# Mixture-of-experts stage of a hybrid decoder block: every expert in blocks of 64 tokens on fp16 halves, weights split one expert ahead

## Chip, cores and metric

The kernel runs on 1 core of a Trainium2 chip. The metric is the device time of one execution in microseconds; of the kernel before there are three runs, and their median counts.

## The reference

One decoder layer over 1024 tokens of width 1024: a mixer (pooling and a state-space scan), then a hierarchical mixture of experts, then a final norm. Only the expert part is touched here. Each token goes to 2 of 32 experts, and an expert is a SwiGLU network with an inner width of 512:

```python
def expert_block(args):
    xb, e = args                       # tokens of expert e
    hu = xb @ w13[e]                   # (n, 1024) @ (1024, 1024)
    a_, b_ = jnp.split(hu, 2, axis=-1)
    return (jax.nn.silu(a_) * b_) @ w2[e]      # (n, 512) @ (512, 1024)
...
out = jax.ops.segment_sum(ys * row_w[:, None], row_tok, num_segments=T)
```

Everything is float32. The router run on the given inputs puts these numbers of tokens on experts 0 to 31: 7, 16, 9, 6, 33, 30, 44, 11, 77, 47, 11, 29, 109, 27, 54, 2, 397, 71, 32, 31, 120, 163, 183, 41, 34, 55, 111, 35, 54, 49, 112, 48. In blocks of 64 that is one block for 23 experts, two for e8, e12, e17, e20, e26 and e30, three for e21 and e22, and seven for e16: 48 blocks, 16 of them behind an expert's first.

## The kernel before

All stages run one after the other; the expert stage is the last long one, a Python loop `for e in range(NE)` written out for 32 experts. The order of instructions on each engine is the order of the code (no scheduler works here), and each engine meets the branches on the token count `rv` by itself.

Weights. An expert has 12 chunks of 512 KB: eight of `w13` (128 rows of the 1024 x 1024 matrix each) and four of `w2`. SP (SyncE) loads them with `load_to` into a ring of `NR` = 39 slots of [128, 1024] float32, 3.25 experts. `Q` = 4 keeps four loads in flight by a dependence, which `lds.clear()` resets. A load waits until the instructions that used its slot are done.

Tokens. The rows of a block are gathered by GpSimd (`gather`, two experts ahead for block 0), transposed by TensorE (`transposed`, tile `px`), and copied by ScalarE to `xa` in float32 (`prep`) or split into fp16 halves `xh` (`parts`).

Halves. A float32 operand can be written as a high and a low fp16 half, `hi = fp16(s*x)` on ScalarE and `lo = fp16(s*x - hi)` on VectorE (`split`, L55 to L59). A product is then three fp16 matmuls (`PASS`): hi by hi, hi by lo, lo by hi.

An expert with at most 64 tokens takes the Else arm (L1287 on): `up64` multiplies `xa` by the raw weights in float32 (64 matmuls of 256 columns), `gated` makes silu times gate (ScalarE, then VectorE, for each half `j`), `turned` transposes that and prepares the next expert's tokens, `refill` gives SP the next eight loads. [...] An expert's block 0 is weighted (`weigh`, VectorE, tile `ye`) and added to the result (`scatter_some`, GpSimd) inside the next expert's turn (`settle`).

An expert with more tokens takes the then-arm (L1264 on): it splits its eight `w13` chunks there, into `P` (two spare slots and its own raw slots, two chunks behind), multiplies two blocks at once with 48 fp16 matmuls of 512 columns (`up128s`), and goes into nested branches (L1282, then `more` with L1221 and L1235) for further pairs; an odd block uses `up64s` (96 fp16 matmuls of 256 columns).

## Time and profile before

| | us |
|---|---|
| median of 3 runs | 1235.07 (1225.71 to 1244.08) |
| profiled execution, own time | 1233.29 |
| its span in the trace | 1231.4 |
| PE (TensorE) busy | 1018.3, 83% |
| DVE (VectorE) busy | 547.8, 44% |
| ACT (ScalarE) busy | 393.0, 32% |
| moved by DMA | 302.82 MB, mean 246 GB/s |
| mean granted TensorE clock | 0.927 of full speed |

The times of all views are microseconds from the start of the span. PE is TensorE's matmul, PEld its weight load, SP the engine that issues the loads. The expert stage fills the stretch from about 534 to 1198; the final norm follows it. A share of busy time over the whole span mixes it with the stages ahead, so the stage is read in stretches of its own.

### The profile page before, as it was taken

The page shows a single profiled execution, that of the slowest core. Times are in us where ns is not written, and L with a number is a line of the kernel's source. Part 1 is how long each engine was busy: PE and PEld are TensorE (multiplying, and loading weights), DVE is VectorE, ACT ScalarE, POOL GpSimd, SP SyncE. Part 2 cuts the span into 40 slices and gives each one's busy share as a digit, 9 for nine tenths or more (in the row PEclk, how much of TensorE's full clock was granted, in tenths as well). Part 3 has the DMA queues.
Part 4 walks back from the last instruction along what each step waited for, and adds up shares of the span by engine and source line. Part 5 has one row for each costly group of instructions (what it writes and reads, how often), then busy time and mean ns, then how long its engine had stood idle before and what let it go on. Part 6 is the DMA issues. An engine that isn't in the chain of part 4 may idle for free.

```text
span 1231.4 us, 20504 instructions
## 1 busy us (share of the span) xinstructions
PE 1018.3 (83%) x7296; PEld 562.5 (46%) x7296; DVE 547.8 (44%) x1168; ACT 393.0 (32%) x747; POOL 253.3 (21%) x253
## 2 busy tenths in 40 slices
PE   4998988989898999667889787789888897797880
PEld 3433435666577555434444443434433343444440
DVE  6763669695788666710004041041413541040325
ACT  6434545465444322200114031041313431140312
POOL 1024324222220103311112121221122211211210
PEclk9998988999999999779989899899988999998995
DMA  9677773132201974789999999995789877999827
GB/s 315 198 193 189 222 226 79 37 80 44 60 1 53 373 283 148 291 275 365 356 355 355 361 374 360 368 367 187 231 272 365 310 233 217 340 369 366 307 31 281
DMA packets 115915, 302.82 MB, mean 246 GB/s; under 512 B 13556, under 2 KB 46506, under 8 KB 115602
## 3 DMA queue, kind: packets, MB, share of 16 engines
q1 hardware_dynamic: 96224, 259.83, 58.3%
q0 software_dynamic: 18160, 39.21, 13.9%
q8 instruction: 111, 1.82, 0.6%
q14 instruction: 202, 1.65, 0.4%
q10 hardware_dynamic: 1218, 0.31, 0.1%
HBM read 275.23 MB, written 24.07 MB: 243 GB/s over the span
## 4 chain that ended last, share of the span: by engine, by line
DMA 36%; PE 34%; issue 13%; DVE 10%; ACT 3%; POOL 2%; POOLq 1%; another core or an unknown queue 0%; DVEq 0%; SPq 0%; ACTq 0%
PE p L53 14%; DMA acc<-ye,idx 13%; DMA xg<-h2tab,idx 13%; PE proj L53 6%; PE po L53 5%; PE zp L53 3%; DMA abc<-acsd 2%; DMA table<-ent,dsti 1%; DMA wo<-in_w_dram 1%; DMA win<-in_w_ada_dram 1%; PE st L53 1%; PE pl L53 1%; DVE raw L1318 1%; DMA xt<-in_x_dram 1%; PE py L53 1%
## 5 line engine op out<-in xcount | busy, mean ns | idle before, releaser
L53 PE MATMUL proj<-hT,whl 128*128 128x512 f16 x768 | 182.9, 391 | 3.4 <-ACT hT L359 1.9
L1160 POOL DMA_INDIRECT acc<-ye,idx x48 | 74.1, 1543 | 238.9 <-DVE ye L1145 173.2
L53 PEld LDWEIGHTS <-whl 128*128 128x128 f16 x768 | 75.3, 100 | 103.4 <-issue 27.7
L1093 ACT ACTIVATE wp<-p 128x128 f32<-128x128 f32 (+1 forms) x37 | 11.4, 309 | 347.7 <-PE p L53 347.7
L1067 POOL DMA_INDIRECT xg<-h2tab,idx x48 | 51.4, 1070 | 312.9 <-PE p L53 176.5
L1145 DVE SCALAR_TENSOR_TENSOR ye<-p,gate,g2h 128x512 f32<-128x512 f32 x48 | 36.0, 750 | 175.1 <-PE p L53 145.2
L53 PE MATMUL p<-raw,xa 128*64 128x256 f32 x600 | 80.4, 421 | 28.3 <-issue 20.4
L53 PEld LDWEIGHTS <-xh 128*128 128x128 f16 (+1 forms) x816 | 66.7, 103 | 78.5 <-issue 10.5
L1094 DVE SCALAR_TENSOR_TENSOR wp<-p,wp 128x128 f32<-128x128 f32 (+1 forms) x37 | 12.3, 331 | 202.0 <-ACT wp L1093 195.3
L53 PEld LDWEIGHTS p<-raw,xa 128*64 128x64 f32 x600 | 54.9, 152 | 55.7 <-issue 42.0
L53 PE MATMUL zp<-wz,hT 128*128 128x192 f16 x768 | 69.3, 247 | 3.6 <-ACT zt L528 3.6
L53 PEld LDWEIGHTS <-hT 128*128 128x128 f16 x768 | 63.9, 99 | 6.4 <-issue 5.7
L53 PE MATMUL p<-wo,xa 128*64 128x256 f32 x368 | 50.9, 431 | 18.6 <-issue 15.7
L53 PE MATMUL po<-wo,yT 128*128 128x512 f16 x252 | 56.9, 379 | 0.0
L1094 DVE SCALAR_TENSOR_TENSOR wr<-p,wr 128x128 f32<-128x128 f32 (+1 forms) x37 | 12.3, 331 | 95.8 <-ACT wr L1093 92.7
L53 PEld LDWEIGHTS p<-wo,xa 128*64 128x64 f32 x368 | 33.4, 154 | 35.7 <-issue 26.5
L53 PE MATMUL p<-raw,xh 128*128 128x512 f16 (+1 forms) x234 | 48.8, 366 | 0.0
L1073 PE MATMUL px<-identf,xg 128*128 128x128 f32 x204 | 30.8, 278 | 14.5 <-DMA xg<-h2tab,idx 14.5
L1093 ACT ACTIVATE wr<-p 128x128 f32<-128x128 f32 (+1 forms) x37 | 11.4, 309 | 97.0 <-PE p L53 96.9
L593 POOL TENSOR_TENSOR abc<-acs,negm 128x768 f32<-128x768 f32 x16 | 24.7, 1606 | 77.6 <-DVE mh L635 77.5
L53 PEld LDWEIGHTS <-yT 128*128 128x128 f16 x252 | 24.7, 100 | 26.3
L53 PE MATMUL p<-yb,xa 128*64 128x256 f32 x224 | 30.6, 410 | 5.3 <-DMA raw<-in_w_dram 3.0
(483 smaller groups left out, 1887.2 us busy)
## 6 DMA issues: line engine op xcount, KB each, us to landing
raw<-in_w_dram SPq DMA_DIRECT2D x160, 512.0 KB
wo<-in_w_dram SPq DMA_DIRECT2D x80, 512.0 KB
yb<-in_w_dram SPq DMA_DIRECT2D x60, 512.0 KB
win<-in_w_ada_dram SPq DMA_DIRECT2D x32, 512.0 KB
yps<-in_w_dram SPq DMA_DIRECT2D x20, 512.0 KB
xc<-in_w_dram SPq DMA_DIRECT2D x19, 512.0 KB
xt<-in_w_ada_dram SPq DMA_DIRECT2D x16, 512.0 KB
win<-in_w_in_dram SPq DMA_DIRECT2D x16, 512.0 KB
```

Source lines behind the costliest of these rows:

```text
L53: return PE.matmul(o, l, r, start=start, stop=stop, skip_group_check=True)
L593: G.tensor_tensor(abc.rearrange("p c (r l) -> p c r l", r=3), acs[:, q2, hs, None].to_broadcast([128, 2, 3, 128]), negm[:, None, None, :]. ...
L1067: lastg[0] = G.indirect_dma_start(out=xg, out_offset=None, in_=h2tab, in_offset=bass.IndirectOffsetOnAxis(ap=ix, axis=0))
L1073: PE.transpose(pv[:, k], xg[:, k * 128:(k + 1) * 128], identf)
L1093: A.activation(sils[j][:, 0:n], p1s[j][:, 0:n], AF.Silu, scale=scale)
L1094: V.scalar_tensor_tensor(sils[j][:, 0:n], p1s[j][:, n:2 * n], scale, sils[j][:, 0:n], op0=ALU.mult, op1=ALU.mult)
L1145: V.scalar_tensor_tensor(y, p2, gt, g2h, op0=ALU.mult, op1=ALU.mult)
L1160: G.indirect_dma_start(out=acc, out_offset=bass.IndirectOffsetOnAxis(ap=ix, axis=0), in_=y, in_offset=None, compute_op=ALU.add)
L1318: V.scalar_tensor_tensor(js[i], ts[i], frs[:, i:i + 1], fnw, op0=ALU.mult, op1=ALU.mult)
```

## The change

All experts now run on fp16 halves, in blocks of 64 tokens.

- `up` (96 fp16 matmuls of 256 columns for a block) takes the place of `up64`, `up64s` and `up128s`; `xa`, `prep`, `more`, `EARLY` and the pairs of blocks are gone.
- `divide(e, ks)` splits chunks of expert e. Chunks 0 to 3 of expert e+1 are split during expert e's block 0 (two ahead of `up`, two between its halves `j`), chunks 4 to 7 at the start of its own turn.
- The halves of a chunk go to a slot that was freed two `w13` chunks before it: `plane[i]` is that slot, `lane[i]` the slot into which load i goes. The number of slots stays the same.
- For every expert, block 0 is finished ahead of the branch. Further blocks are `extra(b)`, nested one in the other, each with a hint at its start for the next branch.
- The hint for the expert's own branch stands at the start of its turn and no longer ahead of `down`.
- All 12 loads of an expert are issued together at its end, in both arms (before: 8 ahead of `down`, 4 behind it).

```diff
     for e in range(NE):
-        W = [ring[(12 * e + k) % NR] for k in range(12)]
-        P = wh + [t.bitcast(F16).rearrange("p (a n) -> p a n", a=2) for t in W[:6]]
+        W = lane[12 * e:12 * e + 12]
+        P = halves(e)
...
+        aim(f"e{e}")
+        divide(e, range(4, 8))
+        if e + 2 < NE:
+            gather(e + 2, 0, tokens(e + 2))
+        if e > 0:
+            weigh(p2s[0], slots(0, e - 1)[1], ys[3 * (e % 2)])
+            scatter_some(e - 1, 0, ys[3 * (e % 2)])
+        divide(e + 1, range(2))
+        up(P, 0, lambda: divide(e + 1, range(2, 4)))
+        turned(gT[0], (lambda: parts(xg0[(e + 1) % 2], 0)) if e + 1 < NE else None)
+        down(W, p2s[0], gT[0])
         with tc.If(rv > 64, preferred_fallthrough_block=True, label=f"e{e}") as br:
-            aim(f"b{e}")
...
+            extra(1)
+            refill()
         with br.Else():
-            fetch_ahead()
-            settle()
-            up64(W, e in (0,))
-            turned(0, 1, nxt)
             refill()
-        lds.clear()
-        if e + 1 < NE:
-            aim(f"e{e + 1}")
-        down(W, p2s[0], 0)
-        load_to(12 * e + 12 + NR)
         lds.clear()
```

The new functions (`refill` now reads `load_to(12 * e + 12 + NR)`):

```python
    idle = list(spare)
    for i in range(12 * NE + 2 * NT + 1):
        lane.append(ring[i] if i < NR else plane[i - NR])
        if i < 12 * NE and i % 12 < 8:
            idle.append(lane[i])
            plane.append(idle.pop(0))
        else:
            plane.append(lane[i])
...
    def up(P, a0, mid=None):
        for j in range(2):
            for k in range(8):
                for n, (a, b) in enumerate(PASS):
                    for h in range(2):
                        mm(p1s[j][64 * h:64 * h + 64, 0:256], xh[a][:, k, a0, :], cols(P[k][:, b], 256 * h + 128 * j, 128),
                           k == 0 and n == 0, k == 7 and n == 2)
            gated(j, 128, INV)
            if mid and j == 0:
                mid()
...
        def extra(b):
            last = b == BLOCKS - 1
            if not last:
                aim(f"e{e}b{b + 1}")
                if b == 1:
                    maybe(e, 2)
                maybe(e, b + 2)
            if b == 1:
                parts(rows(e, 1), 1)
            up(P, 1)
            g, p = gT[b % 2], p2s[1 + b % 2]
            turned(g, None if last else lambda: parts(rows(e, b + 1), 1))
            down(W, p, g)
            put(b, p, ys[1 + b % 2])
            if not last:
                with tc.If(rv > 64 * (b + 1), preferred_fallthrough_block=True, label=f"e{e}b{b + 1}"):
                    extra(b + 1)
```

DVE, the turn of expert 1 when it has one block, before: `ye` is `weigh` of expert 0, `wp` and `wr` are the gated halves, and no chunk is split on this path.

```order
L1145 SCALAR_TENSOR_TENSOR ye_5277<-p_5271,gate_4029,g2h 128x512
L1058 UNCONDITIONAL_BRANCH x2
L1094 SCALAR_TENSOR_TENSOR wp<-p_5267,wp 128x128
L1094 SCALAR_TENSOR_TENSOR wr<-p_5268,wr 128x128
L1264 UNCONDITIONAL_BRANCH
L1171 UNCONDITIONAL_BRANCH
```

DVE, the turn of expert 1 now: rows of L59 of 128x1024 make the low half of a chunk (four of expert 1, then four of expert 2), and the one of L59 into `xh` is that of the next tokens.

```order
L59 SCALAR_TENSOR_TENSOR wo_3868<-wo_4049,wo_3868 128x1024
L59 SCALAR_TENSOR_TENSOR wo_3919<-wo_4053,wo_3919 128x1024
L1126 SCALAR_TENSOR_TENSOR ye_5272<-p_5269,gate_4029,g2h 128x512
L59 SCALAR_TENSOR_TENSOR wo_4049<-x_4044,wo_4049 128x1024
L1065 UNCONDITIONAL_BRANCH
L59 SCALAR_TENSOR_TENSOR wo_4053<-sc_4059,wo_4053 128x1024
L1100 SCALAR_TENSOR_TENSOR wp<-p_5266,wp 128x128
L59 SCALAR_TENSOR_TENSOR x_4044<-sh_4058,x_4044 128x1024
L59 SCALAR_TENSOR_TENSOR sc_4059<-h_4048,sc_4059 128x1024
L1100 SCALAR_TENSOR_TENSOR wr<-p_5267,wr 128x128
L59 SCALAR_TENSOR_TENSOR xh_5265<-px,xh_5264 128x8x64
L1237 COMPARE_AND_BRANCH
```

Eight low halves of 128x1024 and one of `xh` now stand on the path of every expert; two chunks of the next expert stand ahead of the first gated half and two ahead of the second.

PE, the end of expert 0 and the branch of expert 1, before: the last transposes (`pg`, `px`), the hint, `down` (four rows of four matmuls), the count, and the branch.

```order
L1132 MATMUL pg<-identf,wr 128x128
L1264 UNCONDITIONAL_BRANCH
L1171 UNCONDITIONAL_BRANCH
L1350 BRANCH_PREFETCH_HINT
L53 MATMUL p_5271<-raw_4019,vecs 32x512 x4
L53 MATMUL p_5271<-raw_4021,vecs 32x512 x4
L53 MATMUL p_5271<-raw_4020,onesf 32x512 x4
L53 MATMUL p_5271<-raw_4022,onesf 32x512 x4
L1194 TENSOR_LOAD cnt
L1264 COMPARE_AND_BRANCH
```

PE, the same place now, the end of expert 0's block 0: the branch is that of expert 0 itself, and behind it stands the further block.

```order
L1117 MATMUL pg<-identf,wr 128x128
L53 MATMUL p_5269<-raw_4019,vecs 32x512 x4
L53 MATMUL p_5269<-raw_4021,vecs 32x512 x4
L53 MATMUL p_5269<-raw_4020,onesf 32x512 x4
L53 MATMUL p_5269<-raw_4022,onesf 32x512 x4
L1237 COMPARE_AND_BRANCH
L1294 BRANCH_PREFETCH_HINT
L1083 MATMUL px<-identf,xg_5260 128x2x2x32 x2
```

The hint has gone from here; it now stands ahead of the whole block 0 (`up` with its 96 matmuls, the transposes and `down`).

SP, the end of an expert's loads, before: eight loads end the arm, four follow, and then the next expert's branch.

```order
L793 DMA wo_4053<-in_w_dram 128x1024
L1264 UNCONDITIONAL_BRANCH
L1171 UNCONDITIONAL_BRANCH
L1350 BRANCH_PREFETCH_HINT
L793 DMA xc_4045<-in_w_dram 128x1024
L793 DMA xc_4046<-in_w_dram 128x1024
L793 DMA g1b<-in_w_dram 128x1024
L793 DMA h_4047<-in_w_dram 128x1024
L1194 TENSOR_LOAD cnt
```

SP, the same place now: the twelve loads (here the last seven) end the arm.

```order
L794 DMA wo_3834<-in_w_dram 128x1024
L794 DMA wo_3868<-in_w_dram 128x1024
L794 DMA wo_3919<-in_w_dram 128x1024
L794 DMA xc_4045<-in_w_dram 128x1024
L794 DMA xc_4046<-in_w_dram 128x1024
L794 DMA g1b<-in_w_dram 128x1024
L794 DMA h_4047<-in_w_dram 128x1024
L1237 UNCONDITIONAL_BRANCH
L1294 BRANCH_PREFETCH_HINT
L1183 TENSOR_LOAD cnt
```

SP meets one group of loads per expert instead of two.

## Rows read from the trace of the kernel before

**Rows 1.** The page's slices: the span in 40, busy tenths of DMA.

```profile
DMA  9677773132201974789999999995789877999827
```

**Rows 2.** Waits of PE in 534:1200: us in total, times, longest.

```profile
PE p L53 <- issue: 66.6, 32, 4.8
PE p L53 <- DMA raw<-in_w_dram: 9.0, 3, 3.1
```

**Rows 3.** Timeline of PE, one-block experts e28 and e29, their first rows.

```profile
1133.40 1.12 PE L53 MATMUL p<-wo,xa 128*64 128x256 f32 x4 [2.88 <-issue]
...
1149.81 0.71 PE L53 MATMUL p<-x,xa 128*64 128x256 f32 x4 [3.06 <-issue]
```

**Rows 4.** Timeline of PE: a 64-token fp16 block of e16, e17's start.

```profile
865.99 0.52 PE L53 MATMUL p<-h,xh 128*64 128x256 f16 x6
...
870.27 1.15 PE L53 MATMUL p<-raw,xh 128*64 128x256 f16 x18
...
872.44 1.92 PE L53 MATMUL p<-raw,uinc 128*32 128x512 f32 x16
874.18 1.90 PE L53 MATMUL p<-raw,negm 128*32 128x512 f32 x16
...
886.13 0.60 PE L53 MATMUL p<-h,xh 128*128 128x512 f16 x2 [0.69 <-ACT xh L57]
```

**Rows 5.** PE's branches and hints: duration ns min/median/max, first and last start.

```profile
L1264 PEldq COMPARE_BRANCH  x1: 5221/5221/5221, 1144.4 to 1144.4; - x1
L1350 PEldq BRANCH_PREFETCH_HINT  x1: 36/36/36, 1142.9 to 1142.9; - x1
L1282 PEldq COMPARE_BRANCH  x14: 74/350/6014, 670.4 to 1176.2; - x14
L1350 PEldq BRANCH_PREFETCH_HINT  x1: 31/31/31, 655.3 to 655.3; - x1
```

**Rows 6.** Groups by form, 534:1200: busy us, mean ns of one, idle before.

```profile
L59 DVE SCALAR_TENSOR_TENSOR raw<-raw,raw 128x1024 f16<-128x1024 f32 x25 | 29.5, 1220 | 0.3 <-ACT raw L57 0.3
L57 ACT ACTIVATE raw<-raw 128x1024 f16<-128x1024 f32 x25 | 25.9, 1054 | 3.0 <-DVE raw L59 2.2 <-DVE sh L59 0.2
L1145 DVE SCALAR_TENSOR_TENSOR ye<-p,gate,g2h 128x512 f32<-128x512 f32 x48 | 36.0, 750 | 175.1 <-PE p L53 145.2 <-issue 20.7 <-DMA acc<-ye,idx 5.0
L59 DVE SCALAR_TENSOR_TENSOR xh<-px,xh 128x512 f16<-128x512 f32 x19 | 12.6, 686 | 17.4 <-ACT xh L57 17.4
L57 ACT ACTIVATE xh<-px 128x512 f16<-128x512 f32 x19 | 10.9, 609 | 27.9 <-PE px L1073 23.1 <-PE p L53 4.8
L1094 DVE SCALAR_TENSOR_TENSOR wp<-p,wp 128x128 f32<-128x128 f32 x26 | 7.6, 292 | 173.1 <-ACT wp L1093 166.5 <-issue 6.6
```

**Rows 7.** Timeline of SP: 40th load, 200th (e16's eighth), a stop before the 232nd.

```profile
536.62 0.34 SPq L793 DMA_DIRECT2D raw<-in_w_dram  x1
...
790.03 7.49 SPq L793 DMA_DIRECT2D raw<-in_w_dram  x8
...
837.29 0.43 SPq L793 DMA_DIRECT2D h<-in_w_dram  x1
869.86 0.33 SPq L793 DMA_DIRECT2D x<-in_w_dram  x1
```

**Rows 8.** Windows: PE, PEld, DVE, ACT, POOL busy, PEclk, DMA share, GB/s.

```profile
404.00:436.00 32.00, 32.00 (x179) 18.41 (x180) 19.00 (x47) 8.53 (x16) 2.14 (x4) 1.00 1.01 399
536.60:790.00 253.40, 207.10 (x1564) 112.42 (x1560) 43.19 (x67) 43.82 (x107) 43.14 (x35) 0.93 1.00 361
720.00:740.00 20.00, 19.22 (x133) 9.93 (x130) 11.89 (x13) 10.83 (x15) 3.16 (x2) 1.00 1.03 388
780.00:800.00 20.00, 17.01 (x138) 10.50 (x134) 1.62 (x4) 1.88 (x6) 4.54 (x4) 0.91 1.02 375
886.13:1198.50 312.37, 262.06 (x1930) 131.53 (x1930) 91.56 (x117) 84.07 (x178) 58.54 (x43) 0.93 0.83 282
```

**Rows 9.** Timeline of PE, the stage's last matmuls (expert 31, `down`).

```profile
1197.39 1.04 PE L53 MATMUL p<-xc,onesf 128*32 128x512 f32 x8
```

More of the change, by code (lines that the diff above doesn't have):

```diff
@@ L33 @@
 Q = 4
-EARLY = 2
+BLOCKS = 8
 YBF = {2: 2, 3: 3, 5: 4, 6: 5, 7: 6}
@@ L788, in block_kernel @@
     lds = []
+    lane, plane = [], []
     def load_to(n):
@@ L1048, in block_kernel @@
     xg0, xg1, xg2 = ([pd1.tile([128, 512], F32, name=f"xg{n}{i}") for i in range(2)] for n in range(3))
-    xa = pd1.tile([128, 8, 64], F32, name="xa")
     xh = [pd1.tile([128, 8, 2, 64], F16, name=f"xh{i}") for i in range(2)]
-    wh = [t.bitcast(F16).rearrange("p (a n) -> p a n", a=2) for t in spare]
     lastg = [None]
@@ L1145, in weigh, with turned, down @@
         V.scalar_tensor_tensor(y, p2, gt, g2h, op0=ALU.mult, op1=ALU.mult)
-    def turned(b, n, ahead=None, between=None):
-        turn(0, n, b)
-        if ahead:
-            prep(ahead)
+    def turned(g, between=None):
+        turn(0, g)
         if between:
             between()
-        turn(1, n, b)
-    def down(W, p2, b, qs=(0, 2, 1, 3)):
-        for q in qs:
-            down_mm(p2, W, q, gT[b][q % 2][:, 64 * (q // 2):64 * (q // 2) + 64])
+        turn(1, g)
+    def down(W, p2, g):
+        for q in (0, 2, 1, 3):
+            down_mm(p2, W, q, g[q % 2][:, 64 * (q // 2):64 * (q // 2) + 64])
     def scatter(y, ix):
@@ L1184, in block_kernel, with halves, divide @@
     lds.clear()
-    prep(xg0[0])
+    parts(xg0[0], 0)
     rvs[0] = nc.values_load(cnt[0:1, 0:1], min_val=0, max_val=T)
-    aim("e0")
     maybe(0, 1)
+    def halves(e):
+        return [plane[12 * e + k].bitcast(F16).rearrange("p (a n) -> p a n", a=2) for k in range(8)]
+    def divide(e, ks):
+        if e < NE:
+            for k in ks:
+                p = halves(e)[k]
+                split(p[:, 0], p[:, 1], lane[12 * e + k])
+    divide(0, range(4))
     for e in range(NE):
-        W = [ring[(12 * e + k) % NR] for k in range(12)]
-        P = wh + [t.bitcast(F16).rearrange("p (a n) -> p a n", a=2) for t in W[:6]]
+        W = lane[12 * e:12 * e + 12]
+        P = halves(e)
         rv = rvs.pop(e)
@@ L1264, in block_kernel @@
-        with tc.If(rv > 64, preferred_fallthrough_block=True, label=f"e{e}") as br:
-            aim(f"b{e}")
-            for b in (2, 3):
-                maybe(e, b)
-            fetch_ahead()
-            split(xh[0][:, :, 0, :], xh[1][:, :, 0, :], xa, HS)
-            for k in range(EARLY):
-                split(P[k][:, 0], P[k][:, 1], W[k])
-            settle()
-            parts(xg1[e % 2], 1)
-            for k in range(EARLY, 8):
-                split(P[k][:, 0], P[k][:, 1], W[k])
-            up128s(P, 2)
-            turned(0, 2, nxt, lambda: down(W, p2s[1], 1, (0, 1)))
-            def fin():
-                down(W, p2s[1], 1, (2, 3))
-                put(1, p2s[1], ys[1])
-            with tc.If(rv > 128, preferred_fallthrough_block=True, label=f"b{e}") as bb:
-                more(1, fin)
-            with bb.Else():
-                fin()
-                refill()
+        def extra(b):
[15 more added lines that the diff above has]
+                    extra(b + 1)
+            else:
+                with tc.If(rv > 64 * BLOCKS, preferred_fallthrough_block=False):
+                    with tc.For_i(BLOCKS, (rv + 63) // 64) as n:
+                        V.tensor_copy(lix, idxs[1].rearrange("p b e -> p (b e)")[:, bass.ds((n - 2) * NE + e, 1)])
+                        V.tensor_copy(lgt, gates[1].rearrange("p b e -> p (b e)")[:, bass.ds((n - 2) * NE + e, 1)])
+                        fetch(xg2[0], lix)
+                        parts(xg2[0], 1)
+                        up(P, 1)
+                        turned(gT[0])
+                        down(W, p2s[1], gT[0])
+                        weigh(p2s[1], lgt, ys[1])
+                        scatter(ys[1], lix)
@@ L1301, in block_kernel @@
     man.__exit__(None, None, None)
-    fin = [ring[(12 * NE + n) % NR] for n in range(2 * NT + 1)]
+    fin = lane[12 * NE:]
     fnw, ts, js = fin[0], fin[1:NT + 1], fin[NT + 1:]
```

103 lines of the change are left out of this document (11 added, 92 removed).

## Prediction, made before the changed kernel ran

> **What bounds the kernel now.** I read the page's slices first, then PE's waits in the expert stage, then the timelines of PE and SP, and last the windows. The slices show DMA at nine tenths or more for most of the first half of the expert stage (from about 534, slice 18 on) and lower behind it [rows 1]. So the stage has two regimes. Until e16's weights have come, the loads set the pace: from 536.60 to 790.00 the DMA share is 1.00 [rows 8], and the 160 loads from the 40th to the 200th take 790.03 - 536.62 = 253.4 us, 1.584 us each [rows 7]. PE keeps just up with that: in the whole stage it waits for raw chunks 9.0 us, but 66.6 us, in 32 times, for nothing but "issue" [rows 2]. That is one wait per expert, and the branch rows name it: the jump into the Else arm holds PE's queue for 5221 ns though its hint stood 1.5 us ahead (1142.9, then 1144.4), and the next expert's first matmul shows 2.88 or 3.06 us of idle time [rows 3, 5]. From e16's seven blocks on, the ring is full: SP stops from 837.29 to 869.86 [rows 7], and then DMA share is 0.83 [rows 8]; PE and its jumps set the pace to the end. A one-block expert takes 1149.81 - 1133.40 = 16.4 us [rows 3]. The stage's last matmul ends at 1197.39 + 1.04 = 1198.4 [rows 9]; behind it come 33.0 us of scatter and norm, which the change leaves alone.
>
> **The sum, part by part.** I follow the end of the stage through three stretches.
>
> *Prices.* Block of 64 on fp16 halves: e16's odd block shows one, 865.99 to 870.27 + 1.15 = 871.42, 5.43 us for the 96 matmuls, 1.02 to the start of `down` at 872.44, and to 874.18 + 1.90 = 876.08 for `down`, 3.64: 10.1 us in all [rows 4]. A chunk's split: 1.054 on ACT, 1.220 on DVE; tokens' split 0.609 and 0.686; gated half on DVE 0.292; `weigh` 0.750 [rows 6].
>
> *A, to the end of e16's block 0, bound by loads.* Before, the first slot comes free at 536.6, behind e0's first chunk. Now ACT and DVE first split all eight chunks of e0 ahead of the end of its half j=0, and only j=1 frees a plane: 8 x 1.22 = 9.8 us, less 0.6 for float32 matmuls that go, so 545.8 (an estimate). This loss of 9.2 us belongs to the change. Its gain is SP's: one group of twelve loads in place of two groups with a branch between them, and slots that PE frees earlier, as it no longer waits 3 us a jump. Bounds: 1.584 us each as before, or the rate of 720:740 and 780:800, where 388 and 375 GB/s were moved [rows 8]. Weights are 160 x 0.524 = 83.9 MB of the 253.4 x 361 = 91.5 MB moved, 92%; 381.5 x 0.917 = 350 GB/s gives 1.50 us. I take 1.53, nearer to those two windows, as their stretches have no SP stop in them: the 200th load (e16's eighth) issues at 545.8 + 160 x 1.53 = 790.6, which is where it was. Two chunks of e17 are now split ahead of e16's second gated half, so the 208th load counts: + 8 x 1.53 = 802.8, about 5 us to land (four in flight), 1.05 + 1.22 to split, 0.9 for gated half, transpose and copy, 3.64 for `down`: block 0 of e16 ends at about 814. PE hides nothing in this stretch and costs nothing: 10.1 us of PE and 11.8 of DVE (below) per expert stand against 12 x 1.53 = 18.4 of loads.
>
> *B, e16's six further blocks.* Each 10.1; the first also needs its tokens transposed and split behind the branch, as `parts` stands in `extra(1)` itself: 0.66 + 0.61 + 0.69 = 1.95. 60.6 + 1.95 = 62.6, so 876.8, against 886.13 for e17's start before [rows 4]: 9 us earlier, since every pair of blocks there cost a split of tokens and a jump more than its matmuls. Between blocks the next `parts` (0.6 of PE, in `turned`) lies beside the second gated half; if not, it costs 0.4 a block.
>
> *C, e17 to e31, bound by VectorE.* A one-block turn on DVE: 8 x 1.220 + 0.686 + 2 x 0.292 + 0.750 = 11.8; ACT has 8 x 1.054 + 0.609 and four small ones, about 10.1. PE: from the moment when the eighth chunk of e is split, DVE does `weigh`, two low halves, a gated half, two low halves, the second gated half (0.75 + 2.44 + 0.29 + 2.44 + 0.29 = 6.2); then 0.8 to `down` and 3.64: 10.6, so PE has 1.2 us to spare in 11.8. In these the jump must lie. With its hint now a whole block ahead (over 10 us), I price it by L1282, whose hint stood 15 us ahead (655.3 to 670.4): median 350 ns, one of 14 at 6014 [rows 5]; L1264's 5221 is the other end. I take 0.35, which the 1.2 hides, plus one miss of 5. The sum: 15 first blocks x 11.8 = 177; six second blocks x (10.1 + 1.95) = 72.3; two third ones x 10.1 = 20.2; behind each of the seven experts with further blocks (e16 too), the last `weigh` and the four low halves of chunks 4 to 7 stand alone, 0.75 + 4 x 1.22 = 5.6 where 1.2 was hidden: 7 x 4.4 = 30.8; e31 has none behind it, -1.2; the miss 5. Together 304: 876.8 + 304 = 1180.9. Before, the same stretch took 312.3 (886.13 to 1198.4), so it gains 8, far less than the 4.6 us (16.4 - 11.8) that a one-block expert saves by itself: the pairs of blocks lose. Loads are no bound here: 12 loads at 18.4 us would be, but the ring is full at e16 and 3.25 experts ahead, and 7 experts of 24 to 38 us refill it; DMA share was 0.83 at 20.8 us an expert [rows 8] and becomes about 0.86.
>
> The end: 1180.9 against 1198.4, -17.5; span 1213.9, own time 1215.8 (1.9 around the span as before). The profiled run stood at 1233.29 against the median of 1235.07, so 1217.5; I say 1218, -1.4%.
>
> [...]
>
> **Rivals.**
>
> [...]
>
> *2, loads no faster.* At 1.584 A and so everything ends 160 x 0.054 + 0.4 = 9 us later: median 1227. For it: the average of 253 us holds all that disturbs loads, gathers and scatters among them, and these stay.
>
> *3, faster: loads run as in the stage ahead.* In 404:436, weights alone, 399 GB/s [rows 8]; with the 92% it is 1.43 us a load, 17 us less in A; if e16's block 0 comes earlier, so does all behind it. Then no miss either: median 1196. For it: nothing that PE does holds SP any more in A. Against: 388 was the best of the two windows with gathers.
>
> *4, the lookahead costs.* The splits of e+1 stand in ACT's and DVE's order ahead of e's gated halves, and the planes are freed only by a whole expert's last use. If each further block waits 1 us for that order, and each one-block turn 1.5 (ACT's and DVE's wait on each other in a split, which the rows show as 3.0 us in 25), C gives back 16 + 14: median 1248. The change then does nothing.
>
> **How the numbers follow.** Chances: forecast 0.42 (1208 to 1227 with loads from 1.50 to 1.55, a further block from 10.1 to 10.6, no or two misses), rival 1 0.13, rival 2 0.15, rival 3 0.20, rival 4 0.10. The likeliest gives 1218. The range leaves out the lower part of rival 3 and the ends of 1 and 4: 1194 to 1250. Within 2% is about what a measurement of this kernel can tell from no change, 1210 to 1260. Faster: rival 3 and the lower quarter of the forecast, 0.32. Slower: rivals 1 and 4 with the slow loads on top, 0.12. Same: 0.56.
>
> **What would show it.** In the changed profile: 96 matmuls in 5.4 us for every block on PE; PE's jump at L1237 of 0.35 us and not 5, with under 1 us of idle time between `down` and the next `up` in A but for chunks; the eighth load of e16 issued at 786 to 799; further blocks of e16 10 us apart; DVE rows one behind the other in C, with 11.8 us from one-block expert to expert, ACT just behind. Wrong it is if PE's "issue" wait stays at 60 us, if SP waits for PE in A, or if PE waits in C for anything but low halves.

## Result and the profile after

The changed kernel takes 1285.32 us (median of 4 runs, 1282.06 to 1292.59) against 1239.24 of the kernel before beside it: 1.040 times, with an interval of 1.030 to 1.050. It is slower; 1218 and 1194 to 1250 were forecast. The profiled execution took 1282.06 us with a span of 1280.3. The ratios leave out the slower runs of the kernel before in later comparisons and one of hint_end as disturbed, while the medians hold them.

The page's busy times and its slices, changed kernel:

```profile
PE 1008.0 (79%) x9640; PEld 633.6 (49%) x9640; DVE 777.3 (61%) x1403; ACT 582.1 (45%) x906; POOL 268.3 (21%) x253
...
DMA  9677772232105947589999999973699675999827
```

DVE has 229.5 us more than the 547.8 of before, ACT 189.1 more; PE has 10 less of 1018.3. DMA's slices look like those of [rows 1]: nine tenths in the first half of the stage, six to nine behind. The forecast's three stretches, read from the timelines, with two experiments that are told further down (both kernels with the block counts fixed, without any branch):

| us | forecast | after | after, no branches | before | before, no branches |
|---|---|---|---|---|---|
| stage's first gather issues | | 529.46 | 523.48 | 528.42 | 525.18 |
| 40th load issues | 545.8 | 547.33 | 541.3 | 536.62 | 532.8 |
| 200th load issues | 790.6 | 799.22 | 786.8 | 790.03 | 775.1 |
| A: e16's block 0 ends | 814 | 831.05 | 816.40 | | |
| B: e16 ends | 876.8 | 901.08 | 878.3 | 886.1 | 848.4 |
| B alone | 62.6 | 70.0 | 61.9 | | |
| C alone, to e31's `down` (matmuls with `w2`) | 304 | 343.1 | 302.2 | 312.3 | 246.6 |
| stage's last matmul ends | 1180.9 | 1244.18 | 1180.5 | 1198.4 | 1095.0 |
| span | 1213.9 | 1280.3 | 1213.1 | 1231.4 | 1127.8 |

The first row is read as a start line: ahead of it the programs are the same, and executions reach it up to 6 us apart (523.48 to 529.46), so stretches of two programs are best compared from it on.

SP's timeline, the 40th and the 200th load, and PE's, the stage's last matmul (they answer to [rows 7, 9]):

```profile
547.33 0.35 SPq L794 DMA_DIRECT2D h<-in_w_dram  x1
...
799.22 0.33 SPq L794 DMA_DIRECT2D h<-in_w_dram  x1
```

```profile
1243.14 1.04 PE L53 MATMUL p<-yb,onesf 128*32 128x512 f32 x8
```

The 160 loads take 251.9 us, 1.574 each, where 1.53 was forecast and 1.584 measured before. The windows from the 40th load to the 200th and over C, to be held against the second and the last row of [rows 8] (the columns are those given there):

```profile
547.30:799.20 251.90, 189.90 (x2220) 126.00 (x2220) 164.47 (x184) 143.82 (x201) 47.82 (x30) 0.91 1.00 355
901.10:1244.20 343.10, 263.30 (x3102) 170.13 (x3102) 181.39 (x214) 155.46 (x234) 63.98 (x44) 0.93 0.80 271
```

In C PE is busy 263.3 us where it was 262.1: the float32 matmuls that went are made up for by more fp16 ones, three for each product. Nearly all of the 31 us that C grew by (29.5) is PE standing idle. DVE, forecast as the bound, is busy only 181 of 343. So C is bound by no engine that is full, but by the waits between them. PE's, 534:1250 (us in total, times, longest), after [rows 2]:

```profile
PE px L1083 <- DMA xg<-h2tab,idx: 30.7, 9, 7.2
PE pg L1117 <- DVE wr L1100: 27.9, 17, 4.4
PE p L53 <- DVE raw L59: 20.4, 27, 5.1
PE p L53 <- issue: 15.2, 10, 3.6
PE p L53 <- PEq L1237: 9.1, 11, 1.4
PE p L53 <- DVEq L1211: 8.6, 7, 1.3
```

"Issue" fell from 66.6 us to 15.2, as the change's earlier hint (`aim`) should make it. In its place stand three waits that before hardly had: for gathered tokens (30.7; none before), for the second gated half (27.9; 2.1 before), for low halves (20.4 and smaller lines). The hint itself works in most turns. PE's branches of L1237, ns min/median/max (before [rows 5]: 5221):

```profile
L1237 PEldq COMPARE_BRANCH  x40: 74/341/7012, 552.5 to 1241.4; - x40
```

Of these 40, eight end an arm (0.18 to 0.20 us each), and nine are the first branches of experts with more than 64 tokens, which do not jump (0.08). The other 23 are the jumps of the one-block experts: 16 took 0.34 to 0.52 us and seven 1.5 to 7.0. Six of the seven are experts 1, 5, 9, 13, 25 and 29, every one-block expert whose number is one above a multiple of four, and in each of the eight other versions of the changed kernel that keep the hint (below) the same six took 3.6 to 7.0. So these misses go with the expert's place in the program; why every fourth was not found.

PE's timeline of a one-block expert, its successor's start in the last row:

```profile
600.11 5.51 PE L53 MATMUL p<-raw,xh 128*64 128x256 f16 x96 [0.81 <-PEq L1237]
...
608.28 0.30 PE L1117 MATMUL pg<-identf,wr 128*128 128x128 f32 x1 [1.79 <-DVE wr L1100]
...
609.39 1.04 PE L53 MATMUL p<-yb,vecs 128*32 128x512 f32 x8
...
612.93 0.33 PE L53 MATMUL p<-raw,xh 128*64 128x256 f16 x2 [0.78 <-DMA sc<-in_w_dram]
```

The turn is 612.93 - 600.11 = 12.8 us and not 11.8. PE waits 1.79 us for the second gated half `wr`, which stands in DVE's order behind two low halves of the next expert, and 0.8 us at each join of the branch's arms.

The gathers. PE's timeline in C, and GpSimd's beside it (the row of 1107.95 ends at 1109.02, and PE's wait for its data at 1114.56, so its duration is not that of the transfer):

```profile
1107.05 0.33 PE L1117 MATMUL pg<-identf,wp 128*128 128x128 f32 x1
1114.56 1.08 PE L1083 MATMUL px<-identf,xg 128*128 128x128 f32 x4 [7.19 <-DMA xg<-h2tab,idx]
1115.44 0.42 PE L1117 MATMUL pg<-identf,wr 128*128 128x128 f32 x1
1115.79 1.94 PE L53 MATMUL p<-yb,vecs 128*32 128x512 f32 x8
```

```profile
1089.78 2.60 POOL L1139 DMA_INDIRECT acc<-ye,idx  x1 [0.30 <-issue]
1107.95 1.07 POOL L1077 DMA_INDIRECT xg<-h2tab,idx  x1 [15.58 <-PE pg L1117]
```

The tokens that PE waits for from 1107.4 on are asked for only at 1107.95, though in the code the gather stands a turn ahead of the transposes that read it. GpSimd is late, and not because of PE, to which the view ascribes the 15.58: its queue came to this gather only then. Its instructions at the branch show why (ns min/median/max); first the changed kernel, then the one before:

```profile
L1237 POOLq EVENT_SEMAPHORE  x115: 17/43/10539, 536.8 to 1244.3; - x115
L1237 POOLq INC_SWDGE_SEM  x23: 979/1413/2036, 541.9 to 1244.4; - x23
```

```profile
L1264 POOLq EVENT_SEMAPHORE  x69: 17/43/43, 536.4 to 1190.6; - x69
```

At the end of the Else arm GpSimd waits on semaphores. Before, the gather and the scatter stood inside the arms, and there are three such waits for each of the 23 one-block experts, none over 43 ns; now gather and scatter stand just ahead of the branch, and there are five (115 in 23). The longest, 10.5 us, holds the queue from 1090.4 to 1101.0, right behind the scatter of 1089.78; the instruction that closes the arm (INC_SWDGE_SEM, just as long in the kernel before) takes 1.7 more, and counts, branches and a second such instruction (1.66 us from 1103.9 on) the rest to 1107.95. That the two added waits are for that gather and scatter is shown by two versions below: the kernel before with both moved ahead of its branch (before_out) has them too, and the changed kernel with both moved into the arms (arms) is rid of them, in this order:

```profile
L1266 POOLq EVENT_SEMAPHORE  x115: 17/43/8242, 534.8 to 1209.0; - x115
```

```profile
L1241 POOLq EVENT_SEMAPHORE  x69: 17/43/43, 544.5 to 1243.1; - x69
```

### The profile page after: what moved, and what is told of

Read it like the earlier page. It is cut to its first block, busy times and chain, and to the rows that moved or that the text cites. A ratio compares the mean times of both kernels' runs of the same rounds, so it can differ in the third digit from the quotient of the medians.

```text
span 1280.3 us, 25945 instructions
## 1 busy us (share of the span) xinstructions
PE 1008.0 (79%) x9640; PEld 633.6 (49%) x9640; DVE 777.3 (61%) x1403; ACT 582.1 (45%) x906; POOL 268.3 (21%) x253
## 3 DMA queue, kind: packets, MB, share of 16 engines
q0 software_dynamic: 18160, 39.21, 13.5%
q10 hardware_dynamic: 1218, 0.31, 0.1%
## 4 chain that ended last, share of the span: by engine, by line
DMA 51%; PE 17%; issue 12%; DVE 9%; POOLq 3%; ACT 3%; POOL 2%; another core or an unknown queue 2%; SPq 1%; DVEq 0%; ACTq 0%
DMA xg<-h2tab,idx 25%; DMA acc<-ye,idx 18%; PE proj L53 5%; PE po L53 5%; DMA abc<-acsd 3%; PE zp L53 3%; POOLq L1062 2%; DMA table<-ent,dsti 1%; DMA win<-in_w_ada_dram 1%; PE pl L53 1%; DMA win<-in_w_in_dram 1%; PE st L53 1%; DMA adad<-adr 1%; POOL abc L593 1%
## 5 line engine op out<-in xcount | busy, mean ns | idle before, releaser
L53 PEld LDWEIGHTS <-xh 128*64 128x64 f16 x4608 | 271.2, 116 | 145.4 <-issue 76.6
L53 PE MATMUL p<-raw,xh 128*64 128x256 f16 x1572 | 117.0, 295 | 31.8 <-DVE raw L59 15.3
L59 DVE SCALAR_TENSOR_TENSOR raw<-raw,raw 128x1024 f16<-128x1024 f32 x79 | 93.5, 1219 | 21.5 <-ACT raw L57 18.2
L53 PE MATMUL p<-wo,xh 128*64 128x256 f16 x1188 | 89.5, 284 | 19.6 <-issue 5.1
L59 DVE SCALAR_TENSOR_TENSOR xh<-px,xh 128x512 f16<-128x512 f32 x57 | 39.3, 689 | 105.3 <-ACT xh L57 105.1
L57 ACT ACTIVATE raw<-raw 128x1024 f16<-128x1024 f32 x79 | 82.1, 1054 | 29.0 <-DVE raw L59 11.8
L57 ACT ACTIVATE xh<-px 128x512 f16<-128x512 f32 x57 | 34.1, 598 | 101.6 <-PE px L1083 101.6
L53 PE MATMUL p<-yb,xh 128*64 128x256 f16 x636 | 49.9, 281 | 12.5 <-DVE wo L59 2.4
L1083 PEld LDWEIGHTS px<-identf,xg 128*128 128x128 f32 x228 | 27.5, 150 | 60.5 <-issue 59.4
L1117 PE MATMUL pg<-identf,wr 128*128 128x128 f32 x48 | 15.3, 318 | 31.3 <-DVE wr L1100 27.9
```

Of the source, the lines that this page charges most:

```text
L53: return PE.matmul(o, l, r, start=start, stop=stop, skip_group_check=True)
L57: A.activation(hi, src, AF.Copy, scale=scale)
L59: V.scalar_tensor_tensor(lo, src, scale, hi, op0=ALU.mult, op1=ALU.subtract)
L1083: PE.transpose(pv[:, k], xg[:, k * 128:(k + 1) * 128], identf)
L1117: PE.transpose(pgs[j][:, 0:128], sils[j][:, 0:128], identf)
```

## Experiments

Ratios are to the kernel before on the same chip, with their intervals. The first theory (G) was that this wait of GpSimd, with the late gathers behind it, makes the loss. Its rivals: DVE's order (the splits of the next expert stand ahead of e's gated halves), the start of the stage (e0's chunks are freed later), and the hint.

**Gather and scatter in both arms (arms).**

```diff
-        if e + 2 < NE:
-            gather(e + 2, 0, tokens(e + 2))
...
-            scatter_some(e - 1, 0, ys[3 * (e % 2)])
+        def pooled(): (the four lines above)
...
+            pooled()        # first in the then-arm, and first in the Else arm
```

> The changed kernel with the gather of expert e+2 and the scatter of expert e-1 issued inside both arms of the branch (as in the kernel before) and no longer ahead of it; all splits stay. Theory G (GpSimd): in the changed kernel the Else arm's closing instruction on GpSimd waits for the gather and the scatter that were issued just ahead of the branch, so GpSimd needs 15 to 20 us an expert and the gathers come late; then PE's 30.7 us of waits for gathers go, one-block experts come 12.9 us apart, the stage ends near 1203 and the time is 1230 to 1245. Theory S (splits): the halves of the next expert ahead of the gated halves cost it; then the time stays at 1275 to 1290. Theory H (hint too early): also no change.

1275.46 us, 1.038 (1.031 to 1.045). Not what G asks for. PE's waits say why:

```profile
PE px L1083 <- DMA xg<-h2tab,idx: 49.5, 12, 14.7
```

The 14.7 is expert 0's tokens, a wait ahead of the stage's first matmul that ends at 540.5 here (533.4 in the changed kernel, so outside the window there). The other 34.8 us stand against 30.7: the gathers come no earlier, since GpSimd now meets its own jump ahead of them. Behind its branch at 1083.95, for one, its next instruction starts at 1088.89.

**Splits 2 and 3 behind the gated halves as well (arms_late).**

```diff
-        up(P, 0, lambda: divide(e + 1, range(2, 4)))
+        up(P, 0)
         turned(gT[0], ...)
+        divide(e + 1, range(2, 4))
```

> The same, and chunks 2 and 3 of the next expert are split behind both gated halves and the tokens' split, no longer between them. Theory G with the order of ACT and DVE as a second, smaller cost: the 2.9 us between the end of the up matmuls and the first down matmul become 1.0, one-block experts come about 11.8 us apart in place of 12.9, and the time is 10 to 15 us under that of arms. Theory S alone: a gain of 1.9 us for each of 32 experts, 40 to 60 us under the changed kernel, whatever arms gives.

1272.83 us, 1.035 (1.028 to 1.043): no gain to speak of, where G asked for 10 to 15 us and S for 40 to 60. PE's timeline of the same expert shows where it goes:

```profile
605.85 0.52 PE L53 MATMUL p<-raw,xh 128*64 128x256 f16 x6 [0.62 <-DVE raw L59]
607.06 0.52 PE L53 MATMUL p<-raw,xh 128*64 128x256 f16 x6 [0.69 <-DVE raw L59]
```

The 1.79 us for `wr` are gone, and PE waits 0.6 to 0.7 us for each of three or four low halves at the start of `up`. A turn is 616.70 - 603.24 = 13.5 us. ScalarE, VectorE and PE run in a ring here, and a wait taken from one place is met at another.

**And e0 by chunks, so that its slots come free one by one (arms_late_first).**

```diff
-        up(P, 0)
+        up(P, 0) if e else up_first(P)     # k outside, j inside, both gated halves last
```

> The same as arms_late, and expert 0 multiplies each chunk for both halves in turn, so that its first slot comes free some 9 us earlier. If the loads bound the first part of the stage, all of it moves: 7 to 10 us under arms_late, about 1215. If PE or GpSimd bounds it, no change.

1256.33 us, 1.026 (1.016 to 1.035), 16.5 less than arms_late where 7 to 10 were expected, and far from the 1215 named with them. The 40th load issues at 537.2 instead of 548.4 and the 200th at 791.5 instead of 801.8 (2.9 us of both because this execution reached the stage earlier): the loads do bound A, and this term of the forecast holds.

**The kernel before, with gather and scatter put ahead of its branch (before_out).**

```diff
+        fetch_ahead()
+        settle()
         with tc.If(rv > 64, preferred_fallthrough_block=True, label=f"e{e}") as br:
...
-            fetch_ahead()      # in both arms
-            settle()
```

> The kernel before with one thing changed: gather of expert e+2, weighting and scatter of expert e-1 stand ahead of the branch and no longer inside its arms. Theory G: the closing instruction of the arms on GpSimd now waits for them too, one-block experts go from 16.4 to 18 us or more, and the time rises by 20 to 50 us over the kernel before. Theories S and H: within 6 us of the kernel before, since no split and no hint is moved.

1242.95 us, 1.009 (1.005 to 1.014). G's place costs some 11 us there, half of the least expected: clear of no change, and far too small.

**The gather three experts ahead, on the changed kernel (ahead).**

```diff
-        if e + 2 < NE:
-            gather(e + 2, 0, tokens(e + 2))
+        if e + 3 < NE:
+            gather(e + 3, 0, tokens(e + 3))   # xg0 with three buffers
```

> The changed kernel with one difference: block 0 of an expert is gathered three experts ahead and not two, into a third buffer. Theory G in the form that is left after arms (GpSimd's instructions for one expert, with their waits and jumps, take 15 to 20 us, so that gathers come late in any place): PE's waits for gathers (30.7 us) fall under 10 us, and with them the down matmuls at half clock behind such waits; the time is 1240 to 1260. Theory S (the splits in the order of ACT and DVE cost it): within 8 us of the changed kernel.

1282.86 us, 1.042 (1.031 to 1.053): nothing, although the wait is removed. PE's waits, to be held against those of the changed kernel:

```profile
PE pg L1117 <- DVE wr L1100: 42.7, 25, 5.6
...
PE p L53 <- issue: 19.3, 12, 3.9
PE px L1083 <- issue: 13.2, 4, 6.6
PE p L53 <- PEq L1237: 12.7, 9, 5.0
...
PE px L1083 <- DMA xg<-h2tab,idx: 4.6, 1, 4.6
```

The gathers' 30.7 us fell to 4.6. The wait for `wr` rose by 14.8, and the three lines of "issue" and of the branch are 45.2 in all, 15.6 more than the same three of the changed kernel (15.2, 9.1, and 5.3 for `px`). G falls here: late gathers mostly lay over time that PE would have waited anyway.

**Both (best): arms_late_first with the gather three ahead.**

```diff
-                gather(e + 2, 0, tokens(e + 2))
+                gather(e + 3, 0, tokens(e + 3))
```

> arms_late_first with the gather three experts ahead. Theory G: 15 to 25 us under arms_late_first, 1230 to 1242, about the kernel before. Theory S: within 8 us of arms_late_first.

1256.28 us, 1.019 (1.006 to 1.032), as arms_late_first alone, where G asked for 15 to 25 us less.

**best without GpSimd's branch on 32 tokens for block 0 (lean).**

```diff
-                gather(e + 3, 0, tokens(e + 3))
+                fetch(rows(e + 3, 0), slots(0, e + 3)[0])
...
-                scatter_some(e - 1, 0, ys[3 * (e % 2)])
+                scatter(ys[3 * (e % 2)], slots(0, e - 1)[0])
```

> best, and block 0 is gathered and scattered without the branch on more or fewer than 32 tokens, always with all 64 rows (rows past the count come from and go to a spare row). This takes two count loads, two branches and two semaphore instructions from GpSimd's chain of each expert, some 4 us of about 15, and adds transfers for the eleven experts with few tokens. Theory G: 3 to 12 us under best. If the transfers weigh more than GpSimd's chain: the same or slower.

1257.07 us, 1.021 (1.010 to 1.033): no difference. GpSimd's branches on 32 tokens do not set the pace.

**The kernel before, hint for e+1 at the start of the Else arm and at the end of the then-arm (before_hint), and at the end of both (hint_end).**

```diff
         with br.Else():
+            if e + 1 < NE:
+                aim(f"e{e + 1}")
...
-        if e + 1 < NE:
-            aim(f"e{e + 1}")
         down(W, p2s[0], 0)
```

> The kernel before with one difference: the hint for the next expert's branch stands at the start of the one-block arm, ahead of up64, as the changed kernel has it (lead of some 10 us in place of 1.5). If PE's jump is what bounds one-block experts behind e16: the gap of 3 us falls under 1 and the time falls by 10 to 25 us. If GpSimd's chain of 16 us an expert (with a jump of its own of 5 us) bounds them in the kernel before too: within 6 us of the kernel before.

> before_hint with the one-block arm's hint at its end, where the kernel before had it within a few rows, while the arm for more tokens keeps its hint at its own end. In before_hint's trace the one-block jumps still take 4 to 6 us and the time went into the experts with more blocks. If the gain of 27 us came from the place of the hint in that arm, this kernel is as fast as before_hint (1203 to 1216); if from the early hint in the one-block arm, it is as slow as the kernel before (1228 to 1243).

1210.43 us, 0.982 (0.971 to 0.993), and 1202.16 us, 0.979 (0.971 to 0.987). The two have the same order on all engines (the hint stands at the start of its arm in both), so the second is a repetition of the first, and what it was to tell apart stays open. It also shows what single profiles are worth: the two spans, 1210.3 and 1194.2, are of one order of instructions. This is the version that beats both kernels. But the jump is hardly shorter, with the hint some 10 us ahead: 19 of the 23 one-block jumps of before_hint are still over 1 us (22 before). PE's branches at L1264, nine of them at the end of an arm, and one-block experts in PE's timeline, before_hint:

```profile
L1264 PEldq COMPARE_BRANCH  x41: 74/3562/6026, 532.4 to 1162.9; - x41
```

```profile
1114.03 8.81 PE L53 MATMUL p<-wo,xa 128*64 128x256 f32 x64 [3.61 <-issue]
...
1130.59 0.65 PE L53 MATMUL p<-x,xa 128*64 128x256 f32 x4 [3.09 <-DMA yb<-in_w_dram]
```

These experts still take 16.6 us. In hint_end "issue" stands at 48.1 us in 28 waits. What did become shorter is the branches inside the arm for more tokens: those at L1282 had four of 14 at 3.95 to 6.01 us in the kernel before, and has none now:

```profile
L1282 PEldq COMPARE_BRANCH  x9: 74/333/366, 661.8 to 1156.9; - x9
```

From one expert's first `up` matmul to the next one's, the nine experts with further blocks take 302.9 us in all before, 287.9 in before_hint and 288.9 in hint_end; the 23 others take 361.4, 356.3 and 341.1. So 14 to 15 us of the gain stand in the nine, in both. Why the same hint helps one-block jumps there less than in the changed kernel was not found.

**Without low halves of w13 (no_lo); and with the gather three ahead (ahead_no_lo).** Both leave out the low halves of `w13`: the high half is used twice.

```diff
-                split(p[:, 0], p[:, 1], lane[12 * e + k])
+                split(p[:, 0], p[:, 1], lane[12 * e + k], parts=(0,))
```

> The changed kernel without the low halves of w13: only the high halves are made (ScalarE), and the pass that multiplied by the low half multiplies by the high half again, so TensorE has the same matmuls and VectorE 256 instructions of 1.22 us less; part of the computation is left out. Theory D (VectorE's low halves, and the waits between ACT, DVE and PE around them, set the pace behind e16): one-block experts come 10.5 to 11.5 us apart, the stretch from e16's end to the last matmul goes from 343 to 280 to 300 us, the time is 1225 to 1245. Theory G (GpSimd's chain): PE waits for gathers in place of low halves, the stretch stays over 325, the time over 1265.

> ahead (gather three experts ahead) without the low halves of w13, in the same way; part of the computation is left out. If both theories D and G hold, one cover hides the other, and only this run shows it: the stretch behind e16 is 270 to 290 us and under that of no_lo by 10 or more. Theory D alone: as no_lo, within 6 us. If it stays over 320, neither, and jumps and matmuls themselves set the pace.

1270.31 us, 1.032 (1.026 to 1.038), and 1267.14 us, 1.028 (1.022 to 1.034). DVE's eight splits an expert are gone, and only 15 us against the changed kernel, 16 against ahead. C takes some 332 us in either, so theory D (280 to 300) fails, and so does that of both D and G (270 to 290): with both covers away something else sets the pace. ahead_no_lo's timeline shows what PE meets then:

```profile
1094.24 0.55 PE L53 MATMUL p<-yb,xh 128*64 128x256 f16 x6 [2.53 <-PEq L1237]
...
1099.29 1.33 PE L53 MATMUL p<-wo,xh 128*64 128x256 f16 x17 [3.47 <-issue]
```

A missed jump (2.53 us of idle PE), and a second stall of 3.47 us, with nothing to wait for, 25 matmuls behind it.

**Without the hint of the expert's branch (nohint).**

```diff
-        aim(f"e{e}")
         divide(e, range(4, 8))
```

> The changed kernel without the hint for the branch behind block 0. If the hint works and the jump lies on the path (25 of 32 jumps took 0.07 to 0.52 us with it): each one-block expert's jump takes 5 us again and the time rises by 15 to 40 us. If other waits cover the jump: within 8 us of the changed kernel. Theory H (the hint comes too early and harms): faster.

1294.61 us, 1.048 (1.041 to 1.054), some 9 us more than the changed kernel's 1285.32. PE's jumps:

```profile
L1236 PEldq COMPARE_BRANCH  x40: 70/4678/7841, 552.4 to 1253.5; - x40
```

All 23 one-block jumps now take 3.4 to 7.8 us (with the hint, seven of 23 were over 1 us), 136 us in all instead of 38; the 17 other rows did not change. So the early hint works, but 98 us more in jumps cost 9 us in all, less than the 15 expected at least, which is again one wait taking another's place.

**No branches at all (static_after, static_before), and two of the above on top (static_first, static_no_lo).** The token counts stand as numbers in the program, so these four are right for the given input alone; static_no_lo leaves out the low halves of `w13` too. Besides branches, hints, count loads and the instructions that close an arm, they lack the transposes and splits of tokens for a block that no token is in: nine times four transposes in static_after (0.60 us each four, 5.4 us of PE in all), three times four in static_before. Theory C is that the control flow makes the loss: PE's jumps that come late, GpSimd's waits at the end of an arm (up to 10.5 us in the changed kernel) and with them late gathers (PE waits up to 7.2 us for one).

```diff
+    CNT = [7,16,9,6,33,30,44,11,77,47,...]
...
-            rvs[e + 1] = nc.values_load(cnt[0:1, e + 1:e + 2], min_val=0, max_val=T)
+            rvs[e + 1] = CNT[e + 1]
...
-        with tc.If(rv > 64, preferred_fallthrough_block=True, label=f"e{e}") as br:
+        if rv > 64:
```

> The changed kernel with the number of blocks of each expert taken from the given input when the kernel is built: no counts are loaded, no branch, hint or jump and none of the semaphore instructions that close an arm is left on any engine; matmuls, splits, gathers, scatters and loads are the same and in the same order. It is right for this input alone. [...] Theory S (work and order of the splits on ACT and DVE): the stretch stays over 325 and the time over 1260.

> The kernel before in the same way. Its jumps cost PE 3 us for each one-block expert and 2 to 4 at the inner ones: under theory C the stretch behind e16 falls from 312 to 270 to 285 us and the time to 1195 to 1212. The gap to static_after is then what the change of the arithmetic is worth without its control flow: if static_after is the faster, control flow took the gain; if it is the slower, the splits and single blocks lose by themselves.

> static_after with expert 0 multiplying each chunk for both halves in turn, so that its first slot comes free some 9 us earlier. Loads bound the first part in either theory: 8 to 12 us under static_after.

> static_after without the low halves of w13 (the high halves are used in their place; part of the computation is left out). With control flow gone the cover that hid VectorE in no_lo is gone too: if the low halves set the pace of one-block experts (12.9 us against 10.5 to 11), the stretch behind e16 is 25 to 40 us shorter than in static_after; if it is shorter by under 10, they do not.

| | us | ratio to before | C |
|---|---|---|---|
| static_after | 1219.56 | 0.997 (0.992 to 1.001) | 302.2 |
| static_first | 1212.97 | 0.991 (0.987 to 0.995) | |
| static_no_lo | 1189.62 | 0.973 (0.961 to 0.985) | 277.6 |
| static_before | 1130.49 | 0.925 (0.914 to 0.936) | 246.6 |

The windows over C of static_after, static_no_lo and static_before, in this order:

```profile
878.30:1180.50 302.20, 251.41 (x3082) 162.62 (x3078) 176.19 (x208) 150.80 (x228) 74.86 (x44) 0.94 0.85 298
```

```profile
872.40:1150.00 277.60, 240.85 (x3082) 157.08 (x3078) 46.03 (x92) 143.95 (x227) 57.46 (x44) 0.94 0.91 325
```

```profile
848.40:1095.00 246.60, 239.50 (x1922) 114.64 (x1922) 90.11 (x115) 82.79 (x176) 58.90 (x42) 1.00 0.99 360
```

Freed of its branches, the kernel before has PE busy 97% of C at a granted clock of 1.00, with DMA at 0.99: it has hardly anything left to wait for. Its C is 23 us under the 270 to 285 expected, its time 65 under 1195: branches cost far more than PE's idle time at the jumps. The changed one is inside what theory C asked for, 290 to 310 and 1205 to 1235, and still has 51 us of idle PE, none of it for gathers. PE's two longest waits in C, static_after:

```profile
PE pg L1119 <- DVE wr L1102: 23.7, 20, 3.4
PE p L53 <- DVE raw L59: 10.6, 18, 0.7
```

A one-block expert in PE's timeline, static_after (585.26 to the next start) and static_before (1051.10 to the next start, at 1062.82):

```profile
585.26 5.58 PE L53 MATMUL p<-raw,xh 128*64 128x256 f16 x96
...
593.51 0.30 PE L1119 MATMUL pg<-identf,wr 128*128 128x128 f32 x1 [1.79 <-DVE wr L1102]
...
597.31 0.85 PE L53 MATMUL p<-raw,xh 128*64 128x256 f16 x12
```

```profile
1051.10 0.65 PE L53 MATMUL p<-x,xa 128*64 128x256 f32 x4
...
1062.82 0.66 PE L1075 MATMUL px<-identf,xg 128*128 128x128 f32 x4
```

12.05 us against 11.72. The fp16 matmuls save 1.4 us of `up` (5.69 to `pg` against 7.05), and the 1.79 for `wr` takes it back. These are among the shortest turns of either. An expert with two blocks, e20, takes 20.4 us in static_before (892.23 to 912.59) and 25.6 in static_after (932.35 to 957.96). All turns of C, each from an expert's first `up` matmul to the next one's, in us:

| experts of C | static_before | static_after | dearer by | before | after |
|---|---|---|---|---|---|
| nine with one block | 109.7 | 123.6 | 13.9 | 138.8 | 145.1 |
| four with two | 77.4 | 104.7 | 27.3 | 100.8 | 112.2 |
| two with three | 59.5 | 73.9 | 14.4 | 72.7 | 84.5 |

Three quarters of the 55.6 us by which C is dearer without branches stand in the six experts with further blocks, where two blocks at once in the kernel before have become single ones.

static_no_lo prices the low halves, with the branches out of the way, at 24.6 us of C, just under the 25 to 40 expected and twice what no_lo showed with them. It is a lower price: up to e26's start the build without them is 31.6 us ahead, and behind it ScalarE waits for loads, 8.5 us for one at 1097.5. static_first gains 6.6 where 8 to 12 were expected.

## Why the prediction was wrong

**The sum left out what branches cost, and set the rest against a measurement that contains it.** Its stretches are those of static_after within 2.5 us each: A 816.4 for 814, B 61.9 for 62.6, C 302.2 for 304, span 1213.1 for 1213.9. A part of this is luck. That execution reached the stage's first gather 4.9 us before the kernel before did, and from there A takes 292.9 us, not 285.6; C had 5 us for one miss in it, and turns of 11.8 that take 12.05 at least. With its branches the same program needs 67 us more (1280.3 - 1213.1). 6.0 of them lie ahead of the stage's first gather and are not the branches'; 61 are the stage's: 8.7 in A, 8.1 in B, 41 in C, 3.5 behind it. The sum had 5. The failing step is in part C: "In these the jump must lie", 0.35 us hidden in PE's spare 1.2, plus one miss. In C alone three of nine jumps were missed, and joins of arms and late gathers had no term at all.

**Two readings of the rows beside it were wrong.** "That is one wait per expert" is not so: the 32 waits stand beside 22 one-block jumps and eight branches inside the arm for more tokens that took 2.0 us or longer, while the nine experts with more tokens enter that arm in under 0.1 us. And L1282, which priced the hinted jump, was read as one long one in 14; the trace has four, 3.95 to 6.01 us. A row of smallest, median and longest does not say how many are long.

**Before has the same cost, and more of it.** 1231.4 - 1127.8 = 103.6 us, 100.4 of them from the stage's first gather on. So branches became 39 us cheaper with the change. That this is the hint's work is not shown: nohint loses only 9 of it. The arithmetic and its order became 87 us dearer (689.6 - 602.6, both without branches and from the first gather on), and 87 - 39 = 48 is the measured difference of the spans but for 1 us ahead of the stage. The prediction's "4.6 us (16.4 - 11.8) that a one-block expert saves by itself" is this error in one line: 16.4 holds the jump's 3 us of idle time and matmuls at a granted clock of 0.55 behind it (1133.4 to 1137.0), while the work is 11.7; the 11.8 held neither. Like set against like, the change loses 0.3 us on the shortest of these turns and 1.5 in the mean of the nine in C (13.7 for 12.2).

**Step by step.**
- The block of 96 fp16 matmuls in 5.4 us: right (5.5).
- A's start: 547.33 for 545.8, right. static_first and arms_late_first bear the term out.
- Loads at 1.53: without branches 1.534, with them 1.574, nearly as slow as before. That is rival 2, and 7 us. Then e16's block 0 ends 31.8 us behind its eighth load, for 23.4: another 8, of which 6 stand without branches too (29.6). PE waits 3.82 us there for gathered tokens (to 824.48), and without branches 20.8 and 33.9 us in all of A and B for the two gated halves; the sum had no term for these in A. The sum's 5 us for a load to land were the author's estimate, which no row shows: the load four behind e16's eighth, which waits for that one, issued 6.6 us after it (799.22 to 805.81).
- B: 70.0 for 62.6; without branches 61.9.
- C, the turn: 11.8 by DVE's busy time was too low, and DVE is not full even without branches (176 of 302 us). What PE waits for most there is `wr`, behind two low halves in DVE's order; rival 4 named this wait, and gave it 1.5 us for the 1.79 seen (its 16 further blocks are those of the whole stage; C has eight). C itself missed by 39 us. Joins of the arms are 16 of it: PE idles 0.78 us behind a one-block expert and 1.25 behind nested blocks, where the static kernel overlaps by 0.07 (8 x 0.85 + 7 x 1.32).
- Rival 1 of the chances (0.13), the hint that comes too early: no run shows that a lead of a whole block makes a jump as dear as one without a hint. 16 of the 23 jumps took 0.34 to 0.52 us with that lead, where all 23 took 3.4 us or more in nohint; why the other seven took 1.5 to 7.0 was not found.
- Not priced at all: GpSimd's wait at the end of an arm for transfers issued just ahead of the branch. It helped to make gathers late, by up to 7 us for PE, but removing it (arms), or its effect (ahead), gave next to nothing by itself.

**What stays open.** How the 61 us divide among joins (16 in C), missed jumps with their second stalls, late gathers and lower clock: arms, ahead, lean and no_lo each took one away, and others took its place, so they don't add up. Of the 55.6 us by which C is dearer without branches, the low halves are 24.6; the other 31 (blocks of 64 in place of pairs, ScalarE's high halves, their order) were not taken apart. No build without branches had the splits moved behind the gated halves, so whether the order alone loses the 23.7 us for `wr` is not shown.

## What to carry to other kernels

A sum of durations is a forecast of a program without branches; before it is set against a measured time, that time has to be read in the same way, and a build of both kernels with the counts fixed does this in one run (here -1.4% was forecast, +4.0% measured, and +7.9% is between the two builds with counts fixed). When an engine waits in a ring of three, removing its longest wait can show little (30.7 us of gather waits fell to 4.6 in ahead, and the time from 1285.32 to 1282.86): add up the ring, or find the version in which one engine is busy nearly all the time (PE 97% here), and measure the distance to that. Transfers issued just ahead of a branch may be waited for at its end (up to 10.5 us here, none over 43 ns with them inside the arms). And a split that runs ahead for the next step can hold up what the present step is waiting for (`wr`, 1.79 us); moving it behind that only moved the wait here (arms_late: 0.6 to 0.7 us for each of three or four low halves).

## What the runs showed of the hardware

- Branches on the token count cost the kernel before 100 of 1231.4 us and the changed one 61, from the stage's first gather on and against builds with the counts fixed, where PE's own "issue" waits showed 66.6 and 15.2.
- Without a hint all 23 one-block jumps held PE's queue for 3.4 to 7.8 us (nohint). With one a whole block ahead, 16 took 0.34 to 0.52 (the changed kernel); the same six missed in all nine versions that have it, every fourth expert (3.6 to 7.0 us).
- A missed jump can be followed by a second stall: 2.53 us of idle time at the jump and 3.47 us of "issue" 25 matmuls behind it in ahead_no_lo; 1.43 and 1.18 behind expert 29 in the changed kernel. The forecast had one price for a miss.
- Behind the 7.19 us wait for a gather, eight matmuls of `down` took 1.94 us (1115.79), where eight of the same shape took 1.04 at 609.39. The granted clock is 0.50 in the first place and 1.00 in the second (the column ahead of the last two), so the wait came with 0.90 us on top of its length:

```profile
1114.56:1117.70 3.14, 3.14 (x17) 1.49 (x21) 0.69 (x1) 1.44 (x3) 0.00 (x0) 0.50 1.07 326
608.00:610.50 2.50, 2.22 (x21) 0.81 (x25) 0.73 (x2) 1.19 (x2) 0.00 (x0) 1.00 0.98 380
```

- GpSimd's closing of an arm takes 1.0 to 2.0 us (INC_SWDGE_SEM, 23 times, in both kernels), and ahead of it up to 10.5 us of waiting on semaphores where gather and scatter are issued just before the branch (the changed kernel; 8.2 in before_out), none over 43 ns where they stand inside the arms (the kernel before, arms).
